# One core, a hybrid conformer/attention block: accumulation tiles of two PSUM banks, and the score transposes one place later

## The chip, the cores and the metric

The kernel runs on one core of one Trainium2 chip. The metric is the device time of one execution in microseconds (us), the median of several runs. TensorE is called PE here (PEld is its weight load), VectorE DVE, ScalarE ACT, GpSimd POOL, and SyncE, which issues nearly all loads, SP.

## The reference

```python
def hybrid_layer(x, ...):                       # x: 1 x 256 x 2048, float32, one layer
    h = rmsnorm(x, norm_mix_g)
    a, g, q, k, v = split(h @ w_in)             # 1024 columns each
    u = causal_dwconv(a * sigmoid(g), conv_dw_w, conv_dw_b)   # depthwise, width 31
    conv_out = silu(layernorm(u))
    o = diff_attention(q, k, v, lam)            # 8 heads, softmax(s1) - lam * softmax(s2), block-causal
    attn_out = rmsnorm(o, subln_g) * (1 - lambda_init)
    x = x + concat(conv_out, attn_out) @ w_out
    gate, up = split(rmsnorm(x, norm_ffn_g) @ w_up)           # 5632 columns each
    x = x + (gelu(causal_dwconv(gate, width 3)) * up) @ w_down
    return rmsnorm(x, norm_final_g)
```

All of it is float32, with 256 tokens.

## The kernel before, in words

Every large product is made of float32r matmuls on split operands: `split` (L144 to L157) turns each weight chunk that arrives by DMA into a high part (`hi`, a cast on ACT, L151) and a low part (`lo`, a subtraction on DVE, L152), in pieces of four k steps of 256 columns. Activations lie in `xT` as high and low parts too.

`wide_group` (L179) makes 256 output channels for all 256 tokens, as two blocks of 128 channels (n = 0, 1), over 16 k steps. For each k and n PE does `big` (L187: the block's `hi` against the high and low activations, 512 columns) and then `small_` (L190: `lo` against the high activations, 256 columns, added to the second half of the same bank). This is one pair; a group has 32 pairs, 64 matmuls. The written order of a group is big, small, big, small and so on; in the last k step it is small, big for each n. Each block has an accumulation tile of one PSUM bank, from the pool `acc` with four banks (L64, L180). `halves` (L234) empties a block: ACT copies the second half of the bank to SBUF, DVE adds the first half.

The program runs in this order. A first pass (L269 to L295) makes four channel blocks while x and weights arrive, in the four tiles `first`. The convolution stage (L377 to L405) has three further pairs of groups, `pa` and `pg`, whose sums are scaled by `rb1` (one factor per token, spread over the partitions by two small matmuls, L103), gated, and handed to the convolution, whose 31 taps per channel pair run on ACT and DVE beside later groups (`conv_tap`). Then come half of the values (`v_slab`, made by `token_chunk`, matmuls L220 to L222), four pairs of groups for q and k (L536 to L559), the other half of the values, the output projection in two halves, and from L674 the FFN: 22 rounds j of two wide groups, gate and up, 44 groups in all, and at last the down projection.

While q and k groups run, the attention of the pair before goes on beside them, cut into steps that the list `bg` holds: `score` (score matmuls and softmax), `turn` (`flip`, L465: PE transposes the weighted scores, L468), `value` (L480 to L482 and a norm), `put` (`store`: PE transposes the head outputs, L510). `tick` takes one step after every fourth k step, so a group has four places, each eight pairs behind the last.

From L376 to the second half of the values and the first half of the output projection PE's order is the written one (`manual_schedule`, closed by `ordered.close()`). Behind that, in the FFN too, a scheduler puts the instructions of each engine in order before the kernel runs. DVE and ACT are ordered by it throughout. Each engine then executes its list strictly in that order.

Of the kernel before, what the change touches and what calls it, by code (L numbers as in the profile page):

```python
# [16 lines left out]
P = 128  # L17
# [10 lines left out]
def block_kernel(  # L28
# [35 lines left out]
    acc = ctx.enter_context(tc.tile_pool(name="acc", bufs=4, space=PSUM))  # L64
# [78 lines left out]

    def split(raw, k0, nk, ncol, cast):  # L144
# [34 lines left out]
    def wide_group(w, c0, xT, n_conv=None, ready=None):  # L179
        ps = [acc.tile([P, 2, T], F32, name="acc") for _ in range(2)]  # L180
# [21 lines left out]
        return ps  # L202
# [28 lines left out]
    def token_banks(width=XW):  # L231
        return [acc.tile([P, width], F32, name="acc") for _ in range(NT)]

    def halves(dst, ps):  # L234
        nc.scalar.copy(dst, ps[:, 1, :])  # L235
        nc.vector.tensor_tensor(dst, ps[:, 0, :], dst, op=ALU.add)  # L236

    with ph1:
# [10 lines left out]
        first = [acc.tile([P, T], F32, name="acc") for _ in range(4)]  # L249
# [61 lines left out]
        with prio(300):  # L311
            prod = small.tile([P, 2, QK], F32, name="lamp")
            lv = lam_in.rearrange("p (a b) q -> p a b q", b=2)
            nc.vector.tensor_tensor(prod, lv[:, :, 0, :], lv[:, :, 1, :], op=ALU.mult)
            ls = const.tile([P, 2], F32, name="ls")
            nc.vector.tensor_reduce(ls, prod, axis=AX.X, op=ALU.add)
            nc.scalar.activation(ls, ls, AF.Exp)
            nlam = const.tile([P, 1], F32, name="nlam")
            nc.vector.tensor_tensor(nlam, ls[:, 1:2], ls[:, 0:1], op=ALU.subtract)
            nc.vector.tensor_scalar_add(nlam, nlam, -LAMBDA_INIT)  # L320
            sg = const.tile([P, 1], F32, name="sg")
            nc.vector.tensor_scalar_mul(sg, col["sg"], 1.0 - LAMBDA_INIT)
            nrq1 = const.tile([P, NT], F32, name="nrq1")
            nc.vector.tensor_scalar_mul(nrq1, rstd1, -1.0 / math.sqrt(QK))
            mask = p1.tile([P, 3 * P], F32, name="mask")
            nc.gpsimd.memset(mask, 0.0)
            nc.gpsimd.memset(mask[0:CHUNK, CHUNK:P], NEG)
            nc.gpsimd.memset(mask[0:CHUNK, 2 * P + CHUNK : 3 * P], NEG)

# [5 lines left out]
        upad = []  # L335
        cv = [p1.tile([P, 2, T], F32, name=f"cv{j}") for j in range(NP)]
        for j in range(NP):
            u = p1.tile([P, 2, PADW + T], F32, name=f"u{j}")
            nc.gpsimd.memset(u[:, :, 0:PADW], 0.0)
            upad.extend([u[:, 0, :], u[:, 1, :]])  # L340

# [34 lines left out]
        ordered.enter_context(tc.manual_schedule(engines={mybir.EngineType.PE}))  # L376
        for j in range(NP):  # L377
            pa = first[:2] if j == 0 else wide_group(wi, j * GW, xT, n_conv=RATE_A, ready=early if j == 1 else None)
            an, gn = [], []
            for n in range(2):  # L380
                a_ = p2.tile([P, T], F32, name=f"a{n}")
                if j == 0:
                    with prio(ATT):
                        nc.scalar.copy(a_, pa[n])
                else:
                    halves(a_, pa[n])
                nc.vector.tensor_tensor(a_, a_, rb1, op=ALU.mult)
                an.append(a_)
            pg = first[2:] if j == 0 else wide_group(wi, CC + j * GW, xT, n_conv=RATE_A)
            for n in range(2):  # L390
                g_ = p2.tile([P, T], F32, name="g_")
                if j == 0:
                    with prio(ATT):
                        nc.vector.tensor_copy(g_, pg[n])
                else:
                    halves(g_, pg[n])
                nc.vector.tensor_tensor(g_, g_, rb1, op=ALU.mult)
                gn.append(g_)
            for n in range(2):
                c = 2 * j + n  # L400
                g_ = gn[n]
                nc.scalar.activation(g_, g_, AF.Sigmoid)
                nc.vector.tensor_tensor(upad[c][:, PADW:], an[n], g_, op=ALU.mult)
# [15 lines left out]

        v_slab(0, H // 2)  # L420
# [115 lines left out]
        for j in range(H // 2):  # L536
            pq = wide_group(wi, 2 * CC + j * GW, xT, n_conv=RATE_Q)
            qT, kT = [], []
            for n in range(2):
                q_ = p2.tile([P, T], F32, name=f"q{n}")  # L540
                with prio(ATT):
                    halves(q_, pq[n])
                qT.append(q_)
            pk = wide_group(wi, 2 * CC + H * P + j * GW, xT, n_conv=RATE_Q)
            for n in range(2):
                k_ = p2.tile([P, T], F32, name=f"k{n}")
                with prio(ATT):
                    halves(k_, pk[n])
                    nc.vector.tensor_tensor(k_, k_, rb1, op=ALU.mult)
                kT.append(k_)  # L550
# [124 lines left out]
    with ExitStack() as ph2:  # L675
# [116 lines left out]
        with tc.manual_schedule(engines={mybir.EngineType.PE}):  # L792
# [5 lines left out]
            tail = acc.tile([P, hw], F32, name="acc")  # L798
# [86 lines left out]
```

## Time and profile before

| | |
|---|---|
| median of 3 runs | 1085.82 us (1085.8 to 1085.91) |
| the profiled execution | 1085.98 us, of it 1084.2 us are the span of the trace |
| PE busy | 1072.0 us, 99% of the span |
| DVE busy | 781.3 us, 72% |
| ACT busy | 602.6 us, 56% |
| DMA | 205.82 MB, mean 190 GB/s |
| granted TensorE clock | 0.998 of full speed (2.4 GHz) |

Busy time is the union of an engine's instructions. PE's instructions overlap each other, so a busy PE may still issue them more or less densely; the distance from the start of one matmul to the start of the next says how densely. A row of a timeline gives the start from the span's beginning, the duration from the first start to the last end of the merged instructions, and their count after the x.

### The profile page before, as it was taken

What the parts mean: (1) busy time and instruction counts of PE and PEld (TensorE: products, weight loads), DVE (VectorE), ACT (ScalarE), POOL (GpSimd) and SP (SyncE); (2) the same over time, 40 slices, a digit from 0 to 9 for tenths busy, and PEclk for the clock granted to TensorE, in tenths of its full rate; (3) what the DMA queues carried; (4) which work ended last, traced back from release to release, by engine and by line L of the source; (5) the groups of instructions that cost most, each with busy time, mean ns of one, the idle gap of its engine ahead of it and who ended that gap; (6) DMA issues with size and microseconds to landing.
All of it is one profiled execution on the core that took longest, in us unless ns stands there. A gap on an engine that the chain in (4) does not pass through costs nothing.

```text
span 1084.2 us, 15087 instructions
## 1 busy us (share of the span) xinstructions
PE 1072.0 (99%) x5765; PEld 920.7 (85%) x5765; DVE 781.3 (72%) x1257; ACT 602.6 (56%) x986; POOL 11.7 (1%) x33
## 2 busy tenths in 40 slices
PE   9999999999999999999999999999999999999996
PEld 9888888888888888888888888888888888888885
DVE  6799999998877777767777677776777445454544
ACT  7777888887665544544454454544445334343432
POOL 0000000000000000000000000000000000000000
PEclk9999999999999999999999999999999999999999
DMA  9755544445455555555555555555555655555543
GB/s 341 264 186 195 194 156 156 157 155 194 156 197 191 170 185 190 194 194 190 179 183 192 191 194 194 181 177 190 191 195 199 228 194 193 193 194 192 193 173 105
DMA packets 33416, 205.82 MB, mean 190 GB/s; under 512 B 3776, under 2 KB 5568, under 8 KB 10176
## 3 DMA queue, kind: packets, MB, share of 16 engines
q1 hardware_dynamic: 32624, 203.25, 53.5%
q8 instruction: 45, 0.74, 0.2%
q0 software_dynamic: 144, 1.05, 0.2%
q10 hardware_dynamic: 576, 0.57, 0.2%
q14 instruction: 27, 0.22, 0.1%
HBM read 202.75 MB, written 2.10 MB: 189 GB/s over the span
## 4 chain that ended last, share of the span: by engine, by line
PE 94%; DVE 3%; issue 1%; DMA 0%; ACT 0%; SPq 0%; POOLq 0%; POOL 0%; DVEq 0%
PE acc L187 38%; PE acc L190 19%; PE acc L220 11%; PE acc L222 11%; PE acc L221 11%; PE acc L292 2%; DVE cv L355 1%; DVE lo L152 1%; DVE cv L359 1%; DVE pr L445 0%; DMA v_sb<-in_w_in 0%; PE misc L643 0%; DVE pr L459 0%; PE misc L468 0%; PE misc L440 0%
## 5 line engine op out<-in xcount | busy, mean ns | idle before, releaser
L187 PE MATMUL acc<-actT,hi 128*128 128x512 f32 x1856 | 639.9, 396 | 0.0
L152 DVE TENSOR_TENSOR lo<-raw,hi 128x1024 fp32r<-128x1024 f32 x368 | 450.0, 1223 | 251.5 <-ACT hi L151 251.1
L151 ACT CAST hi<-raw 128x1024 fp32r<-128x1024 f32 x368 | 386.8, 1052 | 371.9 <-PE acc L222 167.2
L190 PE MATMUL acc<-actT,lo 128*128 128x256 f32 x1856 | 492.3, 280 | 0.3 <-DVE lo L152 0.3
L187 PEld LDWEIGHTS acc<-actT,hi 128*128 128x128 f32 x1856 | 336.6, 188 | 68.2 <-issue 1.0
L190 PEld LDWEIGHTS acc<-actT,lo 128*128 128x128 f32 x1856 | 350.0, 189 | 15.6 <-DVE lo L152 0.8
L221 PE MATMUL acc<-lo,fT 128*128 128x512 f32 (+1 forms) x355 | 137.5, 387 | 0.0
L222 PE MATMUL acc<-hi,fT 128*128 128x512 f32 (+1 forms) x355 | 137.5, 387 | 0.0
L220 PE MATMUL acc<-hi,fT 128*128 128x512 f32 (+1 forms) x355 | 123.8, 387 | 0.0
L221 PEld LDWEIGHTS acc<-lo,fT 128*128 128x128 f32 x355 | 66.6, 188 | 13.7
L220 PEld LDWEIGHTS acc<-hi,fT 128*128 128x128 f32 x355 | 66.7, 188 | 13.6
L222 PEld LDWEIGHTS acc<-hi,fT 128*128 128x128 f32 x355 | 66.7, 188 | 13.6
L354 ACT ACTIVATE tap<-u,cols 128x256 f32<-128x256 f32 x160 | 71.6, 504 | 6.1 <-DVE cv L355 5.0
L355 DVE TENSOR_TENSOR cv<-cv,tap 128x512 f32<-128x512 f32 x80 | 54.7, 684 | 0.9
L221 PE MATMUL acc<-lo,mixT 128*128 128x512 f32 x128 | 49.8, 392 | 0.0
L222 PE MATMUL acc<-hi,mixT 128*128 128x512 f32 x128 | 49.2, 391 | 0.0
L220 PE MATMUL acc<-hi,mixT 128*128 128x512 f32 x128 | 49.1, 397 | 0.0
L359 DVE SCALAR_TENSOR_TENSOR cv<-u,cols,cv 128x256 f32<-128x256 f32 x80 | 35.1, 478 | 0.3
L235 ACT COPY gp<-acc 128x256 f32<-128x256 f32 x44 | 16.2, 368 | 32.6 <-PE acc L187 32.6
L235 ACT COPY us<-acc 128x256 f32<-128x256 f32 x44 | 16.2, 369 | 24.4 <-PE acc L187 24.4
L236 DVE TENSOR_TENSOR gp<-acc,gp 128x256 f32<-128x256 f32 x44 | 18.6, 422 | 13.8 <-ACT gp L235 13.8
L222 PEld LDWEIGHTS acc<-hi,mixT 128*128 128x128 f32 x128 | 24.0, 188 | 5.2 <-DVE mixT L114 0.2
(195 smaller groups left out, 722.3 us busy)
## 6 DMA issues: line engine op xcount, KB each, us to landing
raw<-in_w_up SPq DMA_DIRECT2D x88, 1024.0 KB, 4.8
raw<-in_w_down SPq DMA_DIRECT2D x43, 1024.0 KB, 4.8
raw<-in_w_in SPq DMA_DIRECT2D x35, 1024.0 KB, 4.8
raw<-in_w_out SPq DMA_DIRECT2D x14, 1024.0 KB, 4.8
mixT<-in_w_in SPq DMA_DIRECT2D x4, 512.0 KB, 8.1
x_sb<-in_x SPq DMA_DIRECT2D x4, 512.0 KB, 10.7
raw<-in_w_out SPq DMA_DIRECT2D x4, 512.0 KB, 3.4
v_sb<-in_w_in SPq DMA_DIRECT2D x5, 256.0 KB, 4.6
```

Source lines behind the costliest of these rows:

```text
L151: cast(hi, src)
L152: nc.vector.tensor_tensor(lo, src, hi.bitcast(F32), op=ALU.subtract)
L187: nc.tensor.matmul(ps[n], lhsT=hi[:, cs], rhs=xT[:, k], start=(k == 0), stop=last)
L190: nc.tensor.matmul(ps[n][:, 1, :], lhsT=lo[:, cs], rhs=xT[:, k, 0, :], start=False, stop=last)
L220: nc.tensor.matmul(ps, lhsT=xT[:, k, 0, ts_], rhs=hi, start=(k == first), stop=False)
L221: nc.tensor.matmul(ps, lhsT=xT[:, k, 0, ts_], rhs=lo, start=False, stop=False)
L222: nc.tensor.matmul(ps, lhsT=xT[:, k, 1, ts_], rhs=hi, start=False, stop=(k == last))
L235: nc.scalar.copy(dst, ps[:, 1, :])
L292: nc.tensor.matmul(first[n], lhsT=w_[:, n * P : (n + 1) * P], rhs=xT[:, kk, x_, :], start=(kk == 0 and w_ is hi and x_ == 0), stop=(k == K ...
L354: nc.scalar.activation(tmp[:, n, :], upad[c][:, k : k + T], AF.Copy, scale=cwcol(k, c))
L355: nc.vector.tensor_tensor(cv[j], cv[j], tmp, op=ALU.add)
L359: nc.vector.scalar_tensor_tensor(cv[j][:, n, :], upad[c][:, k : k + T], cwcol(k, c), cv[j][:, n, :], op0=ALU.mult, op1=ALU.add,)
```

## The change

All accumulation tiles become tiles of two banks, from a pool of two such tiles (the same four banks). A wide group's two blocks lie in one tile `duo`. In the convolution and attention stages both blocks are emptied by one ACT copy and one DVE addition of 512 columns, and scaled, gated and multiplied in one operation each; the FFN still empties them one by one. In the attention list `turn` moves from the sixth of eight places to the seventh, where the `put` of the pair before now goes too, ahead of it; `value` moves from the seventh to the eighth. The first two scalings by `rb1` are ordered behind the first `lo` piece of the next `pg` group, the small products for lambda behind the last gate product, and the text that sets them up is moved down.

```diff
-    acc = ctx.enter_context(tc.tile_pool(name="acc", bufs=4, space=PSUM))
+    acc = ctx.enter_context(tc.tile_pool(name="acc", bufs=2, space=PSUM))
...
-            cast(hi, src)
-            nc.vector.tensor_tensor(lo, src, hi.bitcast(F32), op=ALU.subtract)
+            highs.append(cast(hi, src))
+            lows.append(nc.vector.tensor_tensor(lo, src, hi.bitcast(F32), op=ALU.subtract))
...
-        ps = [acc.tile([P, 2, T], F32, name="acc") for _ in range(2)]
+        duo = acc.tile([P, 2, 2, T], F32, name="acc")
+        ps = [duo[:, 0], duo[:, 1]]
...
-        return ps
+        return duo
...
     def token_banks(width=XW):
-        return [acc.tile([P, width], F32, name="acc") for _ in range(NT)]
+        duo = acc.tile([P, 2, XW], F32, name="acc")
+        return [duo[:, t, :width] for t in range(NT)]
...
-        nc.scalar.copy(dst, ps[:, 1, :])
-        nc.vector.tensor_tensor(dst, ps[:, 0, :], dst, op=ALU.add)
+        nc.scalar.copy(dst, ps[..., 1, :])
+        nc.vector.tensor_tensor(dst, ps[..., 0, :], dst, op=ALU.add)
...
+            scaled.append(nc.vector.tensor_tensor(a_, a_, both_rows(rb1), op=ALU.mult))
+            before_g = len(lows)
+            pg = first[2:] if j == 0 else wide_group(wi, CC + j * GW, xT, n_conv=RATE_A)
+            if j == 1:
+                for s_ in scaled[:2]:
+                    after(s_, lows[before_g])
+                after(gate, highs[before_g + 1])
...
+            q_ = p2.tile([P, 2, T], F32, name="q")
+            with prio(ATT):
+                halves(q_, pq)
...
+            k_ = p2.tile([P, 2, T], F32, name="k")
+            with prio(ATT):
+                halves(k_, pk)
+                nc.vector.tensor_tensor(k_, k_, both_rows(rb1), op=ALU.mult)
...
-                bg.extend([None, score, pending, None, None, turn, value, None])
+                bg.extend([None, score, None, None, None, None, seq(pending, turn), value])
             elif j < H // 2 - 1:
-                bg.extend([None, score, pending, None, None, turn, None, None])
+                bg.extend([None, score, None, None, None, None, seq(pending, turn), None])
...
-                halves(gp[:, FP:], pg[n])
+                halves(gp[:, FP:], pg[:, n])
...
-                halves(us, pu[n])
+                halves(us, pu[:, n])
```

How the change moves instructions is seen at three places. `[waits ...]` names the engines or queues that an instruction waits for.

First, PE in an FFN group, where one piece of four k steps ends and the next begins. Before (L187 is big, L190 small):

```order
L187 MATMUL acc<-actT,hi 128x512
L190 MATMUL acc<-actT,lo 128x256
L187 MATMUL acc<-actT,hi 128x512 [waits Activation_49]
L187 MATMUL acc<-actT,hi 128x512
L190 MATMUL acc<-actT,lo 128x256 [waits DVE_49]
L190 MATMUL acc<-actT,lo 128x256
L187 MATMUL acc<-actT,hi 128x512
```

After (L190 is big now, L193 small):

```order
L190 MATMUL acc<-actT,hi 128x512
L193 MATMUL acc<-actT,lo 128x256
L190 MATMUL acc<-actT,hi 128x512 [waits Activation_49]
L193 MATMUL acc<-actT,lo 128x256 [waits DVE_49]
L190 MATMUL acc<-actT,hi 128x512
L193 MATMUL acc<-actT,lo 128x256
```

Before, the scheduler put both blocks' big matmuls ahead of both small ones at five of the six inner boundaries of each FFN round; after, the written order big, small, big, small stands at all of them, in every FFN group from the third on. In the stages whose PE order is written out, both kernels have the second form everywhere.

Second, PE around the transposes of the third attention pair. Before (L468 are the score transposes):

```order
L190 MATMUL acc<-actT,lo 128x256
L468 MATMUL misc<-ident,pr 128x128 [waits DVE_49] x2
L468 MATMUL misc<-ident,pr 128x128
L468 MATMUL misc<-ident,pr 128x128 [waits DVE_49] x2
L468 MATMUL misc<-ident,pr 128x128
L187 MATMUL acc<-actT,hi 128x512 [waits Activation_49]
```

After (L522 are the output transposes of the pair before, L480 the score transposes):

```order
L193 MATMUL acc<-actT,lo 128x256
L522 MATMUL misc<-ident,osb 128x128 x4
L480 MATMUL misc<-ident,pr 128x128 x3
L480 MATMUL misc<-ident,pr 128x128 [waits DVE_49] x2
L480 MATMUL misc<-ident,pr 128x128
L190 MATMUL acc<-actT,hi 128x512 [waits Activation_49]
```

The score transposes stand eight pairs further down the group, directly behind the output transposes, which before stood four places earlier.

Third, DVE where the first sums are scaled. Before (L387 and L397 scale a and g of the first pass, L152 makes `lo`):

```order
L104 COPY rb_107<-misc 128x256
L320 TENSOR_SCALAR nlam<-nlam 128x1
L387 TENSOR_TENSOR a_494<-a_494,rb_107 128x256
L387 TENSOR_TENSOR a_497<-a_497,rb_107 128x256
L397 TENSOR_TENSOR g__500<-g__500,rb_107 128x256
L397 TENSOR_TENSOR g__503<-g__503,rb_107 128x256
L152 TENSOR_TENSOR lo<-raw,hi 128x1024 x2
```

After (L379 and L393 scale, L154 makes `lo`):

```order
L104 COPY rb_107<-misc 128x256
L154 TENSOR_TENSOR lo<-raw,hi 128x1024
L379 TENSOR_TENSOR a__476<-a__476,rb_107 128x512
L393 TENSOR_TENSOR g__480<-g__480,rb_107 128x512
L154 TENSOR_TENSOR lo<-raw,hi 128x1024
L240 TENSOR_TENSOR a__577<-acc,a__577 128x512
```

One `lo` piece now stands ahead of the two scalings, which were four.

## Rows read from the trace of the kernel before

**Rows 1.** The page's head and its busy time by engine.
```profile
span 1084.2 us, 15087 instructions
PE 1072.0 (99%) x5765; PEld 920.7 (85%) x5765; DVE 781.3 (72%) x1257; ACT 602.6 (56%) x986; POOL 11.7 (1%) x33
```
**Rows 2.** Waits of PE: engine line <- releaser: us in total, times, longest.
```profile
PE misc L468 <- DVE pr L459: 1.7, 2, 1.0
PE acc L190 <- DVE lo L152: 0.3, 1, 0.3
```
**Rows 3.** Timeline of PE, the second pg group: start us, us, instruction [idle before].
```profile
39.88 0.40 PE L190 MATMUL acc<-actT,lo 128*128 128x256 f32 x2
...
40.47 0.62 PE L187 MATMUL acc<-actT,hi 128*128 128x512 f32 x2
41.42 0.39 PE L190 MATMUL acc<-actT,lo 128*128 128x256 f32 x1 [0.34 <-DVE lo L152]
...
51.59 0.40 PE L190 MATMUL acc<-actT,lo 128*128 128x256 f32 x2
```
**Rows 4.** Timeline of DVE at the same place.
```profile
38.34 0.42 DVE L104 COPY rb<-misc 128x256 f32<-128x256 f32 x1 [1.42 <-PE misc L103]
...
38.80 0.76 DVE L387 TENSOR_TENSOR a<-a,rb 128x256 f32<-128x256 f32 x2
...
39.81 0.42 DVE L397 TENSOR_TENSOR g__503<-g__503,rb 128x256 f32<-128x256 f32 x1
40.15 2.35 DVE L152 TENSOR_TENSOR lo<-raw,hi 128x1024 fp32r<-128x1024 f32 x2
```
**Rows 5.** Timeline of PE, the score transposes of three attention pairs, and what follows.
```profile
160.64 0.49 PE L468 MATMUL misc<-ident,pr 128*128 128x128 f32 x3
...
162.41 0.47 PE L187 MATMUL acc<-actT,hi 128*128 128x512 f32 x1
...
188.58 0.49 PE L468 MATMUL misc<-ident,pr 128*128 128x128 f32 x3
...
190.69 0.47 PE L187 MATMUL acc<-actT,hi 128*128 128x512 f32 x1
...
216.86 0.82 PE L468 MATMUL misc<-ident,pr 128*128 128x128 f32 x6
217.44 0.47 PE L187 MATMUL acc<-actT,hi 128*128 128x512 f32 x1
```
**Rows 6.** Timeline of DVE, the operations that these transposes wait for.
```profile
161.41 0.74 DVE L459 SCALAR_TENSOR_TENSOR pr<-pr,sm 128x128 f32<-128x128 f32 x2
...
189.71 0.73 DVE L459 SCALAR_TENSOR_TENSOR pr<-pr,sm 128x128 f32<-128x128 f32 x2
```
**Rows 7.** Windows of three convolution groups and of forty FFN groups: us, busy (count), PEclk, DMA.
```profile
62.88:96.78 33.90, 33.90 (x193) 29.42 (x192) 31.92 (x53) 24.78 (x44) 0.00 (x0) 1.00 0.54 187
386.13:833.73 447.60, 447.60 (x2561) 390.85 (x2560) 326.35 (x520) 220.54 (x321) 0.00 (x0) 1.00 0.54 188
```
**Rows 8.** Timeline of PE, small matmuls three pairs apart, ahead of 51.59 and behind it.
```profile
49.16 0.28 PE L190 MATMUL acc<-actT,lo 128*128 128x256 f32 x1
...
50.20 0.28 PE L190 MATMUL acc<-actT,lo 128*128 128x256 f32 x1
...
53.34 0.28 PE L190 MATMUL acc<-actT,lo 128*128 128x256 f32 x1
...
54.40 0.28 PE L190 MATMUL acc<-actT,lo 128*128 128x256 f32 x1
```
**Rows 9.** Groups by line and form, 42 to 260 us: busy, mean ns, idle before.
```profile
L355 DVE TENSOR_TENSOR cv<-cv,tap 128x512 f32<-128x512 f32 x80 | 54.7, 684 | 0.9
...
L236 DVE TENSOR_TENSOR k<-acc,k 128x256 f32<-128x256 f32 x8 | 3.2, 422 | 0.2
```
**Rows 10.** Timelines of DVE and PE, the last scaling of k and the first score matmuls.
```profile
143.72 0.76 DVE L549 TENSOR_TENSOR k<-k,rb 128x256 f32<-128x256 f32 x2
...
147.72 0.50 PE L437 MATMUL misc<-k,q 64*128 64x128 f32 x4
```

More of the change, by code (lines that the diff above doesn't have):

```diff
@@ L142, in fetch @@
         fetched.append(got)
+    highs, lows = [], []
     def split(raw, k0, nk, ncol, cast):
@@ L248, in block_kernel @@
         wi = w_in
-        first = [acc.tile([P, T], F32, name="acc") for _ in range(4)]
+        firsts = [acc.tile([P, 2, XW], F32, name="acc") for _ in range(2)]
+        first = [d[:, n, :T] for d in firsts for n in range(2)]
         wraw = [
@@ L310, in block_kernel @@
         load_params()
[L311 to L328, printed above, removed]
+        later = []
         def cwcol(k, c):
@@ L376, in block_kernel, with both_rows @@
         ordered.enter_context(tc.manual_schedule(engines={mybir.EngineType.PE}))
+        scaled = []
+        def both_rows(row):
+            return row.rearrange("p (o t) -> p o t", o=1).broadcast_to([P, 2, T])
         for j in range(NP):
             pa = first[:2] if j == 0 else wide_group(wi, j * GW, xT, n_conv=RATE_A, ready=early if j == 1 else None)
[L379 to L382, printed above, removed]
+            a_ = p2.tile([P, 2, T], F32, name="a_")
+            if j == 0:
+                for n in range(2):
@@ L399, in block_kernel @@
[L399 to L403, printed above, removed]
+                        nc.scalar.copy(a_[:, n, :], pa[n])
+            else:
+                halves(a_, pa)
+            scaled.append(nc.vector.tensor_tensor(a_, a_, both_rows(rb1), op=ALU.mult))
+            before_g = len(lows)
+            pg = first[2:] if j == 0 else wide_group(wi, CC + j * GW, xT, n_conv=RATE_A)
@@ new lines, in block_kernel @@
+            if j == 1:
+                for s_ in scaled[:2]:
+                    after(s_, lows[before_g])
+                after(gate, highs[before_g + 1])
+            g_ = p1.tile([P, 2, T], F32, name="g_")
+            if j == 0:
+                for n in range(2):
+                    with prio(ATT):
+                        nc.vector.tensor_copy(g_[:, n, :], pg[n])
+            else:
+                halves(g_, pg)
+            scaled.append(nc.vector.tensor_tensor(g_, g_, both_rows(rb1), op=ALU.mult))
@@ L418, in v_slab @@
                 )
+        with prio(300):
+            prod = small.tile([P, 2, QK], F32, name="lamp")
+            lv = lam_in.rearrange("p (a b) q -> p a b q", b=2)
+            later.append(nc.vector.tensor_tensor(prod, lv[:, :, 0, :], lv[:, :, 1, :], op=ALU.mult))
+            ls = const.tile([P, 2], F32, name="ls")
+            nc.vector.tensor_reduce(ls, prod, axis=AX.X, op=ALU.add)
+            nc.scalar.activation(ls, ls, AF.Exp)
+            nlam = const.tile([P, 1], F32, name="nlam")
+            nc.vector.tensor_tensor(nlam, ls[:, 1:2], ls[:, 0:1], op=ALU.subtract)
+            nc.vector.tensor_scalar_add(nlam, nlam, -LAMBDA_INIT)
+            sg = const.tile([P, 1], F32, name="sg")
+            nc.vector.tensor_scalar_mul(sg, col["sg"], 1.0 - LAMBDA_INIT)
+            nrq1 = const.tile([P, NT], F32, name="nrq1")
+            nc.vector.tensor_scalar_mul(nrq1, rstd1, -1.0 / math.sqrt(QK))
+            mask = p1.tile([P, 3 * P], F32, name="mask")
+            nc.gpsimd.memset(mask, 0.0)
+            nc.gpsimd.memset(mask[0:CHUNK, CHUNK:P], NEG)
+            nc.gpsimd.memset(mask[0:CHUNK, 2 * P + CHUNK : 3 * P], NEG)
+        after(later[0], product)
         v_slab(0, H // 2)
@@ L797, in block_kernel @@
             hw = XW // 2
-            tail = acc.tile([P, hw], F32, name="acc")
+            tail = acc.tile([P, 2, XW], F32, name="acc")[:, 0, :hw]
             k_cut = rest[-CUT][0]
```

31 lines of the change are left out of this document (5 added, 26 removed).

## The prediction

> **What bounds the kernel now.** I read the page's head first: PE is busy 99% of the span, DVE 72% [rows 1]. So only what PE waits for, or the pace at which it issues, can move the end. The waits of PE come next, and they are few: the transposes of the scores wait for DVE, and one `lo` piece comes late [rows 2]. Neither shows the whole loss, because PE's ends overlap the next starts; so I measured both on the timeline, from start to start. The third thing is the pace itself, which busy time hides. Two windows with nothing but wide groups tell it by their counts [rows 7]: three convolution groups put 192 matmuls (96 pairs) into 33.90 us, 353.1 ns a pair or 11.30 us a group; forty FFN groups put 2560 (1280 pairs) into 447.60 us, 349.7 ns a pair or 11.19 us a group. The work of a pair is the same in both, the clock is 1.00 in both, and neither window has a wait of PE. What differs is the order: the convolution groups stand in the written order, the FFN groups have both big matmuls ahead of both small ones at five of six inner piece boundaries.
>
> **Part by part: the first sums.** The second pg group takes from 39.88 to 51.59, 11.71 us [rows 3], 0.41 over the 11.30 of an undisturbed one [rows 7]. On DVE the copy of `rb`, four scalings and only then two `lo` pieces follow each other, and the first piece ends about 41.3 [rows 4]. Its matmul was due at about 40.9: the row at 40.47 holds two big ones, the second starts some 0.22 us behind the first (0.62 less the 0.40 of one), and the small one follows as much later; it starts at 41.42 [rows 3]. In the new order this piece follows the copy, starts near 38.7 and ends near 39.9, ahead of the need. The two scalings behind it are 0.7 us each (an addition of 512 columns has 684 ns [rows 9]), so the next piece ends near 42.5, and its matmul is due eight pairs behind the first, at 43.7. **Term: -0.41 us.** The ends are -0.5 (the wait alone) and nothing.
>
> **The score transposes.** From the first transpose to the next big matmul the three pairs take 1.77, 2.11 and 0.58 us [rows 5]; the third did not wait. So the waits cost 1.19 and 1.53. One place later is eight pairs or 2.83 us. The operations waited for ended at 162.15 and 190.44 [rows 6]; the second half of the transposes was wanted 0.33 us behind the first start, at 160.97 and 188.91, and will be wanted at 163.8 and 191.7. That leaves 1.6 and 1.3 us of slack, if DVE holds its order there, which it nearly does: the list of the changed kernel has the same kinds of work between score and transposes, with one operation of 512 columns for the two additions of q. **Term: -2.72 us.** The ends are 0 and -2.72. The `put` and `value` steps move too. Their number of PE instructions is unchanged; `put` gains four places and so cannot be late, and `value` keeps one place from `turn`.
>
> **The joined operations** take 30 instructions from DVE and 18 from ACT. On DVE two of 256 columns take 0.76 us together and one of 512 has 684 ns [rows 4, 9]. 30 x 0.08 frees some 2.4 us of DVE (and 30 x 0.16 at most, by 2 x 422 ns), which PE waits for at the places above alone: **0 us**. What they cost in lateness: both blocks must be ready before either is emptied, one pair or 0.35 us later. The tightest reader is the first score matmul at 147.72, against the last scaling of k at 144.5 [rows 10]: 3.2 us of slack. A two-bank tile is written again a whole group (11.3 us) after it is left, so its release costs nothing either. The loads keep their order on SP, and POOL gets nothing new.
>
> **The FFN order.** Here the change takes something that nobody asked it to take. With both blocks in one tile the scheduler puts 42 of the 44 FFN groups into the written order, the form that the convolution groups have. The nearest row for such a group is 11.30 us, against 11.19 now [rows 7]: 0.11 us a group, **42 groups, +4.62 us**. The bounds come from the two paces that the trace has: three pairs take 1.04 us (346.7 ns a pair) behind the late `lo`, and 1.06 us (353.3 ns) from the next group end on [rows 8]. At the faster pace throughout, 42 groups of 32 pairs would give back 4.0 us; at the slower they cost 4.9 us. I take the rate of the undisturbed groups, because the faster pace, in written order, did not outlive the end of its group, and the slower one then held over three groups without a break.
>
> A rule of the Trainium skill speaks against this term. The Trainium skill, "TensorE: Matmul & The Clock Gate", section "Back-to-back issue gap", gives the distance of two matmuls by their columns alone (518 cycles for 512, 262 for 256). By that rule a pair costs the same in any order, this term is 0 and the sum is that of the first rival below. Two paces for one kind of pair [rows 7, 8] don't agree with it.
>
> **Sum.** 1085.98 (the profiled execution) - 0.41 - 2.72 + 4.62 = 1087.47 us. That execution lies 0.16 us above the median of the runs, so against 1085.82 I forecast 1087.3 us, 0.14% more. A measurement of this kernel can tell about 0.2% (2.2 us) from no change, so this counts as the same. The bounds of the terms that stand give 1086.8 to 1088.8 (the slower pace, and up to a micro-second of new small waits in the new DVE order); small changes of pace around the moved attention steps are some tenths of a microsecond.
>
> **Rivals.** *The order costs nothing.* The FFN keeps 11.19 us a group, since its pace hangs on something else in that stage (a busier ACT and DVE in the convolution window, 24.8 and 31.9 of 33.9 us [rows 7]). Against it: the pace changed inside one stage, at a group end, with the same neighbours [rows 8]. Time: 1085.82 - 3.13 = 1082.7, faster by 0.29%. Chance 0.18.
>
> *The transposes wait again, one place later.* DVE could bring the last weighted scores later, as more convolution work slips ahead of them; from 163.8 and 191.7 on every microsecond there is one on PE. If both wait as long as now, 2.72 us come back: 1087.3 + 2.7 = 1090.0, slower by 0.39%. Against it stands the slack of 1.3 us and a DVE list with less work. Chance 0.08.
>
> *The faster pace takes hold of the FFN.* The written order at 346.7 ns a pair: 1085.82 - 3.13 - 4.0 = 1078.7. For it speaks only the stretch ahead of 51.59 [rows 8]. Chance 0.03.
>
> *Nothing happens:* the order is free and the transposes wait as before, near 1085.4. Chance 0.04.
>
> **Chances.** My forecast has 0.67. Of it 0.12 lie beyond 1088.0, the bound of slower. So faster is 0.18 + 0.03 = 0.21, the same 0.55 + 0.04 = 0.59, slower 0.12 + 0.08 = 0.20. The likeliest case's own range is 1086.3 to 1088.8; to hold eight in ten the range has to take in the first rival too: 1082.4 to 1088.8.
>
> **What would show it.** Right: PE's waits no longer name the transposes or `lo`; the pg group from about 39.9 on takes 11.3 us; each of the three sets of transposes reaches the next big matmul in 0.6 us (or 1.0 with the output transposes ahead of it, measured from those); a window over forty FFN groups is 452.0 us long, not 447.6. Wrong: FFN groups of 11.19 us (the first rival) or 11.1 us (the third), a transpose with idle time before it (the second), or a wait of PE for a tile's release at a group's start, which I hold for excluded.

## The result, and the profile after

The changed kernel takes **1095.12 us** (median of 5 runs, 1095.04 to 1095.4) against 1085.82 before (1085.8 to 1086.56): ratio 1.0083, interval 1.0072 to 1.0093. It is 9.3 us slower; the forecast was 1087.3 and its range ended at 1088.8. The page's head and its busy time, to set beside [rows 1]:

```profile
span 1093.3 us, 15084 instructions
PE 1080.1 (99%) x5765; PEld 923.9 (85%) x5765; DVE 780.4 (71%) x1227; ACT 596.0 (55%) x968; POOL 11.6 (1%) x33
```

The span has grown by 9.13 us, and PE is still busy 99%. To see where, I cut both spans at three starts on PE's timeline: the first matmul of the second half of the values, of the FFN, and of the down projection. The cut is used for every kernel below.

| stretch | before, us | after, us | difference | forecast |
|---|---|---|---|---|
| start to second half of the values | 223.07 | 221.65 | -1.42 | -3.13 |
| from there to the FFN | 119.31 | 124.72 | **+5.41** | 0 |
| FFN | 493.66 | 498.31 | **+4.65** | +4.62 |
| down projection to the end | 248.14 | 248.63 | +0.49 | 0 |

So the FFN term came as forecast. The rest of the loss lies in the second stretch, for which the prediction had no term. PE's waits, beside [rows 2] (engine, line <- releaser: us in total, times, longest):

```profile
PE acc L223 <- ACT mixT L113: 1.6, 1, 1.6
...
PE acc L223 <- DVE x_sb L750: 0.8, 1, 0.8
PE acc L225 <- DVE mixT L114: 0.6, 1, 0.6
PE misc L449 <- DVE mx L457: 0.5, 2, 0.3
...
PE acc L225 <- DVE mixT L618: 0.3, 1, 0.3
```

The score transposes and the late `lo` piece of [rows 2] are gone. Five other waits stand in their place, and I take them in the order of time. First what went as forecast: PE's timeline at the two ends of the second pg group [rows 3], and at the score transposes of the three pairs [rows 5].

```profile
39.83 0.40 PE L193 MATMUL acc<-actT,lo 128*128 128x256 f32 x2
...
51.12 0.40 PE L193 MATMUL acc<-actT,lo 128*128 128x256 f32 x2
...
162.95 0.82 PE L480 MATMUL misc<-ident,pr 128*128 128x128 f32 x6
163.52 0.48 PE L190 MATMUL acc<-actT,hi 128*128 128x512 f32 x1
...
190.59 0.82 PE L480 MATMUL misc<-ident,pr 128*128 128x128 f32 x6
191.17 0.48 PE L190 MATMUL acc<-actT,hi 128*128 128x512 f32 x1
...
218.21 0.82 PE L480 MATMUL misc<-ident,pr 128*128 128x128 f32 x6
218.78 0.48 PE L190 MATMUL acc<-actT,hi 128*128 128x512 f32 x1
```

The group takes 11.29 us, not 11.71, and each set of six transposes runs on in one row and reaches the next big matmul in 0.57 or 0.58 us. Now the score matmuls of the next pairs (L449 and L452; before L437 and L440), one of the two places:

```profile
173.41 0.50 PE L449 MATMUL misc<-k,q 64*128 64x128 f32 x4
...
174.39 0.59 PE L452 MATMUL misc<-k,q 64*128 64x256 f32 x2
175.31 0.49 PE L449 MATMUL misc<-k,q 64*128 64x128 f32 x2 [0.33 <-DVE mx L457]
...
176.16 0.50 PE L190 MATMUL acc<-actT,hi 128*128 128x512 f32 x1
```

and the same place in the kernel before:

```profile
175.12 0.50 PE L437 MATMUL misc<-k,q 64*128 64x128 f32 x4
...
176.74 0.50 PE L187 MATMUL acc<-actT,hi 128*128 128x512 f32 x1
```

The four score tiles take 2.75 us from the first matmul to the next big one, before 1.62. PE waits ahead of the fourth tile. At the next pair it is 2.62 against 1.61 (201.06 to 203.68, before 203.41 to 205.02). That is 2.1 us of the 2.72 that the transposes had given.

Then the output projection. PE's timeline behind the last output transposes, and the granted clock in two windows there (columns as in [rows 7]):

```profile
258.25 1.10 PE L522 MATMUL misc<-ident,osb 128*128 128x128 f32 x4
...
262.38 0.50 PE L223 MATMUL acc<-hi,mixT 128*128 128x512 f32 x1 [1.63 <-ACT mixT L113]
262.72 0.40 PE L224 MATMUL acc<-lo,mixT 128*128 128x512 f32 x1
263.67 0.79 PE L225 MATMUL acc<-hi,mixT 128*128 128x512 f32 x1 [0.55 <-DVE mixT L114]
264.26 0.63 PE L223 MATMUL acc<-hi,mixT 128*128 128x512 f32 x1
264.69 0.63 PE L224 MATMUL acc<-lo,mixT 128*128 128x512 f32 x1
```
```profile
258.00:264.00 6.00, 3.81 (x15) 2.16 (x14) 5.95 (x12) 5.26 (x13) 0.69 (x1) 0.96 0.50 152
264.00:267.00 3.00, 3.00 (x8) 2.32 (x8) 1.42 (x2) 0.00 (x0) 0.00 (x0) 0.51 0.72 268
```

PE waits for `mixT`, the split head outputs, which ACT (L113) and DVE (L114) make from those transposes; it pauses twice, and then the granted clock is 0.51, the lower of its two levels (1.2 GHz): a matmul every 0.43 us where 0.23 is usual. The time from start to start, less the usual 0.23 a matmul, is lost in these places: 1.80, 0.72 and 0.36 at the waits and right behind them, 1.2 in the six matmuls from 264.26 to 266.82, and 0.51 at the transposes (0.86 to the next matmul, before 0.35). That is 4.6 us of the 5.4. ACT and DVE are late in the main because the convolution still runs there. ACT's timeline, and the line of the convolution's additions on DVE (duration ns min/median/max, first and last start), after and before:

```profile
259.74 0.98 ACT L342 ACTIVATE tap<-u,cols 128x256 f32<-128x256 f32 x2
260.55 1.20 ACT L512 ACTIVATE osb<-misc,sso 128x128 f32<-128x128 f32 x4
261.55 0.78 ACT L113 ACTIVATE mixT<-misc,sg 128x512 fp32r<-128x512 f32 x1
```
```profile
L343 DVE TENSOR_TENSOR cv<-cv,tap x80: 667/684/694, 47.5 to 261.9; 128x512 f32<-128x512 f32 x80
```
```profile
L355 DVE TENSOR_TENSOR cv<-cv,tap x80: 667/684/694, 47.3 to 255.2; 128x512 f32<-128x512 f32 x80
```

The convolution starts 0.2 us later and ends 6.7 us later. The rows of ACT show a second thing: the scaling of the next pair's outputs (L512) takes 1.00 us ahead of L113. In the kernel before it stands behind L113, which only waits for the transposes (L510):

```profile
260.30 0.69 ACT L113 ACTIVATE mixT<-misc,sg 128x512 fp32r<-128x512 f32 x1 [0.74 <-PE misc L510]
260.92 1.14 ACT L500 ACTIVATE osb<-misc,sso 128x128 f32<-128x128 f32 x4
```

Two smaller places remain: 0.46 us near 302 (PE starts 302.42 and 303.11, a wait for DVE's `mixT`), and the tail:

```profile
1079.76 0.39 PE L225 MATMUL acc<-hi,fT 128*128 128x512 f32 x1
1080.93 0.50 PE L223 MATMUL acc<-hi,fT 128*128 128x512 f32 x1 [0.78 <-DVE x_sb L750]
```

The first matmul of the last slab's second block waits until DVE has read the first block, which now lies in the same tile. PE loses 0.94 us there, of which 0.49 reach the end.

The FFN window of forty groups, to set beside the second row of [rows 7]: 452.00 us, 11.30 a group.

```profile
391.85:843.85 452.00, 452.00 (x2561) 392.46 (x2560) 328.24 (x521) 216.55 (x320) 0.00 (x0) 1.00 0.53 186
```

What I should have asked the trace of before is DVE's share where the steps are moved, not on the whole span. Windows of before, then of after:

```profile
150.00:200.00 50.00, 48.14 (x291) 41.50 (x290) 49.29 (x117) 45.34 (x119) 2.82 (x2) 1.00 0.44 155
200.00:250.00 50.00, 50.00 (x272) 41.81 (x271) 49.28 (x113) 42.84 (x99) 0.00 (x0) 1.00 0.43 146
```
```profile
150.00:200.00 50.00, 49.67 (x303) 43.45 (x302) 48.34 (x111) 43.80 (x109) 2.57 (x2) 1.00 0.45 159
200.00:250.00 50.00, 49.80 (x272) 41.57 (x270) 48.28 (x109) 42.13 (x97) 0.31 (x1) 1.00 0.44 148
```

DVE is busy 98.6 of these 100 us before. After, it is busy 96.6 with less of the convolution done; it idles 2 us more, most of it until ACT has copied k or cast a `hi` piece.

### The profile page after: what moved, and what is told of

It is laid out like the page before. It is cut to its first block, busy times and chain, and to the rows that moved or that the text cites. A ratio compares the mean times of both kernels' runs of the same rounds, so it can differ in the third digit from the quotient of the medians.

```text
span 1093.3 us, 15084 instructions
## 1 busy us (share of the span) xinstructions
PE 1080.1 (99%) x5765; PEld 923.9 (85%) x5765; DVE 780.4 (71%) x1227; ACT 596.0 (55%) x968; POOL 11.6 (1%) x33
## 4 chain that ended last, share of the span: by engine, by line
PE 95%; DVE 2%; ACT 1%; issue 1%; DMA 0%; POOL 0%; SPq 0%; POOLq 0%; DVEq 0%
PE acc L190 39%; PE acc L193 20%; PE acc L225 11%; PE acc L223 11%; PE acc L224 11%; PE acc L297 2%; DVE lo L154 0%; ACT hi L153 0%; DMA v_sb<-in_w_in 0%; PE misc L651 0%; PE misc L452 0%; ACT tap L342 0%; PE misc L449 0%; DVE cv L347 0%; DVE cv L343 0%
## 5 line engine op out<-in xcount | busy, mean ns | idle before, releaser
L190 PE MATMUL acc<-actT,hi 128*128 128x512 f32 x1856 | 652.3, 398 | 0.0
L154 DVE TENSOR_TENSOR lo<-raw,hi 128x1024 fp32r<-128x1024 f32 x368 | 450.3, 1224 | 274.2 <-ACT hi L153 273.0
L193 PE MATMUL acc<-actT,lo 128*128 128x256 f32 x1856 | 512.0, 281 | 0.0
L190 PEld LDWEIGHTS acc<-actT,hi 128*128 128x128 f32 x1856 | 345.2, 188 | 80.7 <-issue 0.7
L193 PEld LDWEIGHTS acc<-actT,lo 128*128 128x128 f32 x1856 | 350.6, 189 | 5.2
L223 PE MATMUL acc<-hi,fT 128*128 128x512 f32 (+1 forms) x355 | 137.6, 388 | 0.8 <-DVE x_sb L750 0.8
L225 PE MATMUL acc<-hi,fT 128*128 128x512 f32 (+1 forms) x355 | 137.5, 387 | 0.0
L223 PE MATMUL acc<-hi,mixT 128*128 128x512 f32 x128 | 51.5, 404 | 1.6 <-ACT mixT L113 1.6
L225 PE MATMUL acc<-hi,mixT 128*128 128x512 f32 x128 | 51.1, 399 | 0.9 <-DVE mixT L114 0.6
L225 PEld LDWEIGHTS acc<-hi,mixT 128*128 128x128 f32 x128 | 24.4, 191 | 6.9 <-DVE mixT L114 1.0
L223 PEld LDWEIGHTS acc<-hi,mixT 128*128 128x128 f32 x128 | 24.5, 192 | 6.7 <-ACT mixT L113 2.1
L224 PEld LDWEIGHTS acc<-lo,mixT 128*128 128x128 f32 x128 | 24.4, 191 | 4.8
L223 PE MATMUL acc<-hi,actT 128*128 128x512 f32 x64 | 25.0, 391 | 0.0
```

The source lines that it names most:

```text
L154: lows.append(nc.vector.tensor_tensor(lo, src, hi.bitcast(F32), op=ALU.subtract))
L190: nc.tensor.matmul(ps[n], lhsT=hi[:, cs], rhs=xT[:, k], start=(k == 0), stop=last)
L193: nc.tensor.matmul(ps[n][:, 1, :], lhsT=lo[:, cs], rhs=xT[:, k, 0, :], start=False, stop=last)
L223: nc.tensor.matmul(ps, lhsT=xT[:, k, 0, ts_], rhs=hi, start=(k == first), stop=False)
L224: nc.tensor.matmul(ps, lhsT=xT[:, k, 0, ts_], rhs=lo, start=False, stop=False)
L225: nc.tensor.matmul(ps, lhsT=xT[:, k, 1, ts_], rhs=hi, start=False, stop=(k == last))
```

## The experiments

Theories: **A**, the order of big and small sets the pace of a group (rival **B**: the tiles or the other engines set it). **C**, from 150 to 262 us PE waits where a full DVE and ACT let it wait, and the two edits of order (places of `turn`, `put` and `value`; later first sums) moved those waits to the score matmuls and to the output projection (rival **D**: the joined operations or the tiles did). The stretches of every kernel, from its profiled execution, beside the median of its runs and the ratio to the runs of the kernel before that were made beside it (their medians lie between 1085.82 and 1086.27):

| kernel | to values 2 | to FFN | FFN | to end | median | ratio (interval) |
|---|---|---|---|---|---|---|
| before | 223.07 | 119.31 | 493.66 | 248.14 | 1085.82 | |
| after | 221.65 | 124.72 | 498.31 | 248.63 | 1095.12 | 1.0083 (1.0072 to 1.0093) |
| e1 | 222.59 | 119.32 | 498.40 | 248.12 | 1090.52 | 1.0043 (1.0031 to 1.0056) |
| e2 | 221.92 | 124.81 | 492.69 | 248.64 | 1088.55 | 1.0026 (1.0016 to 1.0035) |
| e3 | 226.07 | 119.96 | 498.32 | 248.61 | 1094.2 | 1.0070 (1.0056 to 1.0084) |
| e4 | 223.01 | 121.89 | 498.32 | 248.64 | 1093.44 | 1.0068 (1.0056 to 1.0081) |
| e5 | 223.19 | 121.37 | 498.31 | 248.65 | 1093.42 | 1.0065 (1.0053 to 1.0078) |
| e6 | 221.90 | 121.52 | 493.67 | 248.12 | 1087.55 | 1.0015 (1.0006 to 1.0024) |
| e7 | 223.00 | 119.29 | 489.50 | 248.15 | 1081.89 | 0.9959 (0.9947 to 0.9972) |
| e8 | 223.14 | 119.36 | 491.81 | 248.11 | 1084.22 | 0.9981 (0.9972 to 0.9989) |
| e9 | 222.01 | 121.18 | 498.32 | 248.64 | 1091.8 | 1.0048 (1.0034 to 1.0062) |
| e10 | 222.33 | 124.64 | 498.32 | 248.10 | 1094.15 | 1.0071 (1.0057 to 1.0085) |
| e11 | 223.04 | 119.28 | 489.51 | 248.13 | 1081.74 | 0.9955 (0.9942 to 0.9967) |
| e12 | 226.17 | 120.23 | 489.64 | 248.08 | 1082.66 | 0.9973 (0.9962 to 0.9984) |
| e13 | 224.38 | 121.52 | 498.31 | 248.63 | 1094.82 | 1.0082 (1.0068 to 1.0096) |
| e14 | 225.57 | 119.56 | 493.66 | 248.13 | 1088.79 | 1.0028 (1.0018 to 1.0039) |

Executions of one kernel spread by some tenths to 3.4 us (e12), so a median can lie a microsecond and more from what the stretches give. The changed kernel, e2 and e10 are the same up to the FFN, and their first stretches differ by 0.7 us, their second by 0.2.

### The pace of the FFN: e1, e2

e1 is the kernel before with PE's FFN order written out:

```diff
+        written = ExitStack()
+        written.enter_context(tc.manual_schedule(engines={mybir.EngineType.PE}))
         for j in range(DFF // GW):
...
+        written.close()
         gf = shared.tile([P, D], F32, name="actT")
```

> The kernel before, with PE's order in the FFN fixed to the written one (big, small, big, small at every piece boundary); nothing else is touched. Theory A, the order sets the pace: 43 groups go from 11.19 to 11.30 us, +4.7 us, 1090.5 us. Theory B, the pace hangs on the two-bank tiles or on what the other engines do there: the groups stay at 11.19 and the time at 1085.8.

Measured: 1090.52, the FFN 498.40 us. A holds to a tenth.

e2 is the changed kernel, with both bigs ahead at the piece boundaries of the FFN groups:

```diff
+                if form and k % 4 == 0 and k > 0:
+                    for n in range(2):
+                        big(n, False)
+                    for n in range(2):
+                        small_(n, False)
+                else:
                     for n in range(2):
...
```

> The changed kernel, with both big matmuls written ahead of both small ones at the piece boundaries of the FFN groups. Theory A: the groups return to 11.19 us or a little less, -4.6 us, 1090.5 us; what stays is the loss ahead of the FFN (about +4 us) and at the tail (+1). Theory B: 11.30 us a group and 1095.1 stay.

Measured: the FFN 492.69 us, 1.0 below the kernel before, where all six inner boundaries of a round have the form and not five. That fits the groups of the kernel before: those with the form at all three boundaries take 11.16 us, those without it at the last one 11.22. The other stretches are those of the changed kernel. The median fell by 6.6 where the FFN gives 5.6. B is out: one order gives one pace with either kind of tile.

### The stall in the output projection: e3, e4, e5, e9

e3 puts the steps back:

```diff
-                bg.extend([None, score, None, None, None, None, seq(pending, turn), value])
+                bg.extend([None, score, pending, None, None, turn, value, None])
...
```

> The changed kernel with turn, value and put back at their places of before. Its ACT list has the last convolution tap two hi pieces earlier than the changed kernel's, level with the kernel before. Theory C, the stall in the output projection comes of a convolution that ends late, and the places made most of that: the stall near 260 us goes (about -5), the stalls between the score matmuls go (about -1.8), the score transposes wait again (+2.7): 1091.0 us. Theory D, the later first sums or the joined evictions made the stall: it stays, the transposes wait again, 1096 to 1098.

Measured: the stretch to the FFN falls to 119.96, and no wait for `mixT` near 260 nor between the score matmuls is left, as C said. But the stretch before it grows to 226.07. The score transposes wait again, now at the second and the third pair, and behind the longer pause the clock falls to 0.58 (PE's waits, then a window):

```profile
PE misc L480 <- DVE pr L471: 3.0, 2, 2.0
```
```profile
218.00:222.00 4.00, 3.71 (x12) 3.13 (x13) 3.87 (x7) 2.08 (x5) 0.00 (x0) 0.58 0.75 262
```

Both stretches together take 346.03 us, in the changed kernel 346.37: what left one place came up at another. The median is 0.9 us lower and the intervals of the two ratios overlap; C's 1091.0 is missed, and so is D's 1096.

e4 frees the first sums:

```diff
-                for s_ in scaled[:2]:
-                    after(s_, lows[before_g])
-                after(gate, highs[before_g + 1])
```

> The changed kernel without the three orderings that put the first scalings and the first gate behind the first pieces of the next group. Its ACT list has the taps one hi piece earlier from the start of the convolution to its end. Theory C says the convolution ends some 3 us earlier, most of the stall near 260 goes: -2.5 to -4.5, and the late lo piece is back: +0.4; 1091 to 1093. If the first sums have nothing to do with the stall: 1095.5.

Measured: the stretch to the FFN falls by 2.8 us, the one ahead of it grows by 1.4. Only one wait of 1.6 us for DVE's `mixT` is left near 260, without a drop of the clock. The late `lo` piece is back, and the longest wait between score matmuls has grown from 0.3 to 0.8 us. The convolution's place in the lists does set this stall, as C has it.

e5 undoes both edits:

> The changed kernel with both edits of order undone (first scalings free, turn, value and put at their old places); what is left of the change are the two-bank tiles and the joined operations. Its lists have the convolution taps level with the kernel before. Theory C, only the two edits of order made the convolution late: no stall near 260 us, the score transposes wait about as before (2.7 us in all), and against before there stay the FFN order (+4.6), the tail (+0.5) and a few tenths: 1091 us. Theory D, the joined evictions make waits of their own: 1093 or more, with new waits between 100 and 260 us.

Measured: the score transposes wait as before (1.7 us in the waits, as in [rows 2]) and the first stretch is that of before within 0.12 us. To the FFN it takes 121.37, so 3.35 of the 5.41 us belong to the two edits of order. The 2.06 left lie in a wait for ACT's `mixT` (0.9 us) and the places around it, and in the 0.46 near 302. D keeps this part, unless the order of ACT's list makes it. The convolution ends as early as before here (the last addition starts at 255.6), but ACT still scales the next pair's outputs ahead of L113, for 1.0 us: more than the wait.

e9 leaves the places and takes work away:

```diff
-            for k in range(CONV_K):
+            for k in range(CONV_K if j < NP - 1 else CONV_K - 6):
```

> The changed kernel with the last six of the 31 taps of the last channel pair left out (this part of the convolution is not computed), so that ACT has 4 us and DVE some 4.6 us less to do before the output projection; all places and orderings stay as in the changed kernel. Theory C, PE stalls near 260 us because ACT and DVE are still busy with the convolution there: the stall goes, the stretch from the second half of the values to the FFN falls from 124.7 to about 120 us, and the time to some 1090.5 us; the stalls between the score matmuls stay. If the stall comes of the moved places in another way (the transposes or their copies late by themselves): it stays, 1094 to 1095.

Measured: 121.18 us to the FFN, 3.5 less; of the wait for ACT's `mixT` 0.6 is left, and the clock stays at full speed. C is right on the larger part; the 120 that I expected was 1 us too low, and what is left above the 119.3 of before is about as large as what e5 leaves. Here too the scaling of the next pair's outputs stands ahead of L113.

### The two terms alone, on the kernel before: e6, e14

```diff
-                bg.extend([None, score, pending, None, None, turn, value, None])
+                bg.extend([None, score, pending, None, None, None, turn, value])
...
```

> The kernel before with turn one place later and value behind it, nothing else; put stays. The prediction's term alone: the two waits of the score transposes go, -2.7 us, 1083.1. Theory E, the waits move: the fourth score tile takes the buffer of the first of its own set (its list waits for DVE there, before for ACT), 0.5 to 1 us at two places, and the last tap stands one hi piece later in ACT's list, so that the convolution ends some 3 us later and what slack there is at the output projection goes: 1084.5 to 1087.

Measured: 1087.55, a ratio of 1.0015 where the prediction's term alone would be 0.9975, and half a microsecond above E's range. In the profiled execution (1086.99, the fastest of eleven) the first stretch gives 1.17 us, the second takes 2.21. PE's waits:

```profile
PE acc L222 <- DVE mixT L114: 1.9, 1, 1.9
...
PE misc L437 <- DVE mx L445: 0.4, 2, 0.2
```

The transposes are gone from the list; the score matmuls and the output projection have come in. With one-bank tiles and single operations, these are two of the changed kernel's new waits. That settles where the gain of `turn` went: to these two places.

e14 orders the first scalings and gates alone:

```diff
+                for s_ in scaled[:4]:
+                    after(s_, lows[before_g])
+                for s_ in gates[:2]:
+                    after(s_, highs[before_g + 1])
```

> The kernel before with the four first scalings behind the first lo piece of the second pg group and the first two gates behind its second hi piece, nothing else. The prediction's term alone: -0.4 us, 1085.4. Theory C: the convolution starts one to two hi pieces later in the lists and stays so until the third attention pair, where it has caught up; -0.4 at the group, and the score transposes wait up to 2 us longer, because DVE has the taps of before still to do: 1086 to 1088.

Measured: 1088.79, above C's range. The wait of the second pg group is gone, but the score transposes wait 3.4 us, not 1.7, and as in e3 the clock falls behind the longer pause:

```profile
PE misc L477 <- DVE pr L468: 3.4, 2, 2.1
```
```profile
218.00:221.50 3.50, 3.50 (x12) 2.90 (x13) 3.43 (x6) 1.84 (x5) 0.00 (x0) 0.54 0.74 290
```

### What is left: e13, e10

e13 is e5 with evictions, scalings, gates and products block by block again, so that of the change only the tiles are left, beside the moved text and SBUF tiles that hold both blocks (the ordering of the small products for lambda is gone too):

```diff
-                halves(q_, pq)
+                for n in range(2):
+                    halves(q_[:, n], pq[:, n])
...
```

> The changed kernel with both edits of order undone as in the fifth experiment, and the evictions, scalings, gates and products done block by block as before: of the change only the two-bank tiles are left. If the joined operations make the 2 us that the fifth kernel lost between the second half of the values and the FFN (121.4 us against 119.3), the stretch returns to 119.3 to 119.8 and the time to 1091.4. If the tiles make them: 121.4 and 1093.4 stay. In its list of ACT the last taps stand two hi pieces earlier than in the kernel before.

Measured: neither. The lists moved once more, with the last taps earlier in them: no stall near 260, but waits of the score transposes (3.0 us at three places) and of a score matmul for DVE's k (1.1 us). So the other 2 us of e5 can't be divided between tiles, joined operations and the order of ACT's list, and this stays open. That order is not the tiles' alone: e14, with one-bank tiles, has the scaling ahead of L113 too. Only the pause near 302 is clean: every kernel with two-bank tiles has it (0.46 us), none with one-bank tiles has.

e10 gives the last slab two tiles:

```diff
-        pd = token_banks()
+        pd = [token_banks()[0] for _ in range(NT)]
```

> The changed kernel with the two blocks of the last down slab in two accumulation tiles instead of one. If PE's pause near 1079.8 us (0.95 us) comes of the shared tile, it goes; since the stretch from the down projection to the end is 148.6 us against 148.1 before, 0.5 us of it are on the end: 1094.6. If it is the read of x itself, nothing changes: 1095.1.

(The lengths in this expectation should read 248.6 and 248.1.) Measured: the pause is gone, the last stretch is 248.10, 0.53 less. The shared tile makes it.

### The pace used: e7, e8, e11, e12

e7 is e1 with the last k step of an FFN group big, small too:

```diff
+                if form and k == KD - 1:
+                    for n in range(2):
+                        big(n, False)
+                        small_(n, True)
+                else:
...
```

> The kernel before with PE's FFN order fixed to the written one, as in the first experiment, and the last k step of a group big, small too, so that big and small alternate without a break. If the turn of the last step (small, big) is what throws the issue into the slower pace, the pace of 347 ns a pair holds: 43 groups at 11.1 us, 1081 to 1083 us. If the pace of the written order is 353 ns whatever the last step is: 1090.5, as in the first experiment.

Measured: **1081.89**, faster than both kernels. PE's timeline in the FFN:

```profile
403.66 0.39 PE L185 MATMUL acc<-actT,hi 128*128 128x512 f32 x1
403.89 0.28 PE L189 MATMUL acc<-actT,lo 128*128 128x256 f32 x1
...
406.78 0.39 PE L185 MATMUL acc<-actT,hi 128*128 128x512 f32 x1
```

Nine pairs in 3.12 us are 347 ns a pair, the faster pace of [rows 8], now held through all groups: the stretch is 8.9 us shorter than in e1. The two differ in the last step of each group alone.

e8 writes every k step big, big, small, small:

> The kernel before with all 16 k steps of each FFN group written as big, big, small, small. If every such piece resets the pace as the piece boundaries of the kernel before do: 347 ns a pair or less, 11.1 us a group, 1082. If the switch costs something of its own each time: 350 ns or more, 1086 to 1091.

Measured: 491.81 us, between the two.

e11 takes the form of e7 into every wide group:

> The kernel before with big and small in turn without a break in every wide group, those of the convolution, q and k too. The FFN gives 4.1 us as in the seventh experiment. If the stretch before the FFN is bound by PE's pace: 14 more groups at 0.2 us, 1079 us. If it is bound by ACT and DVE: the 2.9 us come back as waits of PE (score transposes, output projection), 1081 to 1082.

Measured: the same as e7 in every stretch. That does not show what PE's pace is worth before the FFN, because of the 14 further groups only those of the convolution went faster. PE's timeline in one of them, then in a q group:

```profile
64.85 0.39 PE L185 MATMUL acc<-actT,hi 128*128 128x512 f32 x1
...
67.97 0.39 PE L185 MATMUL acc<-actT,hi 128*128 128x512 f32 x1
...
120.99 0.40 PE L185 MATMUL acc<-actT,hi 128*128 128x512 f32 x1
...
124.17 0.40 PE L185 MATMUL acc<-actT,hi 128*128 128x512 f32 x1
```

Nine pairs take 3.12 us at the first place and 3.18 at the second, 353 ns a pair. The q and k groups alternate without a break too, but the first of them begins at the slower pace, behind the values, and keeps it. Three convolution groups took 33.28 us where e7 has 33.90; this execution had come to them 0.8 us later than e7's, so that the sum of the stretch came out the same by chance. PE's waits at the score transposes are 1.9 us in both. Whether a faster pace there would come back as waits stays open.

e12 is the changed kernel with that form in every group, and e10's tail:

> The changed kernel with big and small in turn in every wide group and the tail of the tenth experiment. FFN 498.3 to 489.5 us (-8.8), the tail -0.5, up to -2.9 in the groups before the FFN; the convolution's last tap stands one hi piece earlier in ACT's list than in the changed kernel, so part of the stall near 260 goes (-1 to -3). 1081 to 1085 us; the stalls between the score matmuls and the pause near 302 us stay, so it does not fall below the kernel of the eleventh experiment.

Measured: 1082.66. Its profiled execution was 3.2 us longer than the median; in it PE idled 1.3 us between score matmuls, and behind that the clock fell:

```profile
178.00:184.00 6.00, 6.00 (x18) 4.61 (x18) 4.91 (x19) 3.27 (x14) 0.00 (x0) 0.50 0.37 156
```

With its order mended, the changed kernel comes to within 1 us of e7 and e11, and not below.

## Why the prediction was wrong

**The FFN order** was right, in cause and size: +4.65 measured, +4.62 forecast, and e1 makes it on the kernel before. The Trainium skill, "TensorE: Matmul & The Clock Gate", section "Back-to-back issue gap", gives the distance by the columns; e7 and e1 have the same matmuls and lie 8.9 us apart in the FFN, so the traces do not agree with it. One sentence there took too much from its rows: that the faster pace, in written order, did not outlive the end of its group. What ended it in the FFN was the last step, turned round to small, big; without that the pace holds (e7).

**The first sums** gave 0.4 us at their place, as forecast. But the step "the next piece ends near 42.5" was where I stopped asking. On DVE the same work stands later from there on, and in e14 that alone makes the kernel 2.9 us slower.

**The score transposes** are the step that failed: the term of -2.72 was booked as time off the end. The transposes did stop waiting, with the slack that I had worked out. But for "the list of the changed kernel has the same kinds of work between score and transposes" I asked only whether the moved step would be late, and not who is served later for it. I had read DVE as 72% of the span [rows 1]; between 150 and 250 us it is at 98.6%, with ACT at 88. New waits came where PE next needs DVE or ACT: at the score tiles (2.1 us) and at the output projection, where the convolution ended 6.7 us later and PE's pauses cost 3.4 us with the late transposes, and the lower clock 1.2 more. That PE's old waits were time in which a full DVE caught up is an argument and not shown: in the changed kernel DVE itself idles more there, 3.4 us and not 1.4. e6 shows the move of the waits with `turn` and `value` alone: 1.0 us of span lost instead of 2.72 gained. The Trainium skill, "Perfetto Trace Analysis", section "Optimization Strategy", says that a kernel can have regimes in which the most-contended engine changes, and to look within the regime; these windows agree with it.

**The moved `value`** was costed at nothing, since it "keeps one place from `turn`". It also holds a PSUM tile of the pool `misc`, and now it stands two places ahead of the next scores, before three. In the lists the fourth score tile waited for ACT before, whose norm reads what `value` made; in the changed kernel and in e6 it waits for DVE, and PE's trace names L457, DVE's reading of the score tiles. I had looked at the release of the accumulation tiles and not at that of the tiles beside them.

**The joined operations** at 0 us: they free DVE of work, but in the changed kernel DVE idles 1.2 us for ACT's joined copy of k between 150 and 250 us. That is not theirs alone, for e6 with its single copies shows the same 1.2 us (its groups by line, 150 to 250 us), and e5, with joined ones at the old places, 0.4:

```profile
L240 DVE TENSOR_TENSOR k<-acc,k 128x512 f32<-128x512 f32 x3 | 2.1, 692 | 1.4 <-ACT k L239 1.2
```
```profile
L236 DVE TENSOR_TENSOR k<-acc,k 128x256 f32<-128x256 f32 x6 | 2.4, 426 | 1.2 <-ACT k L235 1.2
```

Up to 2 us of the loss may be theirs, the tiles' or the order of ACT's list; that is the open part.

**The shared tile** I held for excluded as a wait, and looked for it only at a group's start. It stands inside the last slab: 0.49 us on the end, shown by e10.

Of the rivals, the second had the right sign, but less than half the size and another mechanism: the transposes did not wait again. The bound of "up to a micro-second of new small waits in the new DVE order" had no row behind it, and it is the number that failed: outside the FFN the kernel lost 7.6 us against the sum (1.7 in the first stretch, where a gain of 3.1 was forecast and 1.4 came, 5.4 in the second, 0.5 at the end).

## What to carry to other kernels

Before you take a wait away, read the busy share of the engine waited for in that stretch: if it is near 100%, the wait may be that engine's work showing, and then it can come up at the next place, as in e6. Read the order of the other engines' lists there too. When a step moves, follow every tile that it holds, those of other pools too. And when a pool or a tile changes, compare the order of the matmuls: with the work the same, the order of big and small alone was worth 8.9 us in the FFN, more than all else in this change.

## What the runs showed of the hardware

The same pairs of matmuls, at full clock and with no wait, ran at about 347 or 353 ns a pair. In unbroken alternation either pace lasted: 347 through the FFN of e7, 353 in the q group of e11 above. What changed it in these traces was a break of the alternation, or a pause ([rows 8], behind the late `lo` piece). With the last step turned round at each group's end the FFN ran at 353 (e1, and the changed kernel). In the kernel before, the third quarter of an FFN group ran at 352 and the fourth at 348 where it began with both big matmuls, at 354 where it did not.

The granted clock fell to about half in the changed kernel behind two pauses of PE close together (1.63 and 0.55 us idle), in e3 and e14 behind one of 2.0 and one of 2.1 us, in e12 behind one of 1.3. In the kernel before, with a pause of 1.0 us, in e13, with one of 1.4, and in e4 and e6, with one of 1.6 and one of 1.9, the windows behind it show 1.00. So the length of a pause alone did not tell whether the clock fell; where it did, matmuls of 0.23 us came every 0.43 us for some 3 to 7 us more.
